# Cutting an output projection and its gate by token halves, with one half between attention blocks

## The chip, the cores and the metric

The kernel runs on one core of a Trainium2 chip. The metric is device time in microseconds, from the first instruction to the end of the program; lower is better. The profile comes from one profiled execution, and its span runs from the first to the last instruction of the program.

## The reference

One layer of a hybrid decoder trunk over 1024 tokens of width 1024. With `A = 512`:

```
xn = rms_norm(x, mix_norm)
q, k, v, gate_a, u, gate_s = split(xn @ w_in)             # six parts of 512
attn = dilated_mixture_attention(q, k, v) * silu(gate_a)  # 8 heads, windows (128,1) (512,4) (2048,16)
ssm  = s5_glu(u, ...) * silu(gate_s)                      # scan, GELU, GLU with w_glu
h    = x + concat(attn, ssm) @ w_out
gate = sigmoid(rms_norm(h, ple_norm) @ w_ple_gate)
out  = h + gate * (p @ w_ple_proj)                        # p: 256 wide
```

All arithmetic is fp32 in effect: each operand of a large product is split into a rounded high part and a remainder, and three products are summed (`mm3`).

## The kernel before

Most tiles are feature major: 128 features by 512 tokens, two token halves `n`. The stages, in the order of the program: the u projection, the state space heads woven with the two gate projections (SiLU, stored to `sg_s` and `sa_s`), q and k, v, the GLU, the output projection in two parts ("s": the four ssm rows of `w_out`, both token halves; "a": the four attention rows), the statistics of h, and the embedding gate with the embedding projection.

Attention is a Python generator (L754) over eight blocks of 128 query tokens. Its loop takes 4 heads at a time in block 0, 2 in block 1 and 1 in the others, so it has 2, 4 and 8 steps a block, 54 in all. A step is: scores on TensorE into a bank "s" (L793; blocks 4 to 7 have far keys too, L750), a row minimum on VectorE (L780), Exp on ScalarE (L803), the split in two fp16 parts by VectorE, ScalarE and GpSimd (L807 to L810), a transposing DMA (`pt<-hl`), and the product with v on TensorE (L818, L824). At the end of blocks 2, 3, 6 and 7 the finished blocks are transposed, gated and split into `ma` (two buffers of 4x512 for each token half).

`step(n)` advances the generator n steps at the place where it is called: 8 steps in v, 5 in the GLU (`GS`), 2 or 3 after each of the 16 tiles of part "s" (`OS`, 16 + 24). Tile's scheduler makes one fixed order for each engine from priorities and its own estimate of times; `high_priority` moves instructions ahead. Semaphores do the rest: an engine that waits holds everything behind it in its order. All DMAs are issued by SP, in one order.

Part "s" evicts x + 0.5 times the product and stores it to `h_s`; part "a" loads that, adds its product and makes `hh`, `hl` (high part and remainder of h) and the sum of squares. `load_w` (L146) loads a 128x512 weight tile through a ring of raw buffers (`RAW`: three, and two from the GLU on), makes the high part on ScalarE (L157, L160) and the remainder on VectorE or GpSimd (L158, L161), in 8 slots each. Part "s" and part "a" have 8 such tiles each, the gate 16, the embedding projection 4. The gate multiplies each weight tile with both token halves. Large buffers of the GLU and the output projection come from one pool of six (`quad`, tag "mx"). PSUM has the banks "big" (2), "s" (3), "t" (2) and "pv" (1).

## Time and profile before

| | |
|---|---|
| time, median of 3 runs | 690.49 us (690.44 to 690.92) |
| span of the profiled execution | 686.2 us |
| TensorE matmul busy | 630.0 us (92%) |
| VectorE busy | 496.8 us (72%) |
| ScalarE busy | 289.5 us (42%) |
| GpSimd busy | 302.0 us (44%) |
| mean granted TensorE clock | 0.968 |
| DMA | 87.25 MB, mean 127 GB/s |

The profiled execution's time is its span and what lies around it; the median of the runs is 4.3 us above the span. Busy times are unions over an engine's instructions. Matmuls are pipelined, so a stretch in which TensorE is busy throughout can hold more or fewer of them; the number of matmuls stands beside it.

### The profile page before, as it was taken

The numbers are of one execution on the slowest core, as the hardware profiler recorded it, in microseconds if no ns is written. First come the engines' busy times: TensorE is split into PE (matmuls) and PEld (weight loads), VectorE is DVE, ScalarE is ACT, GpSimd is POOL, SyncE is SP. The second block draws the span as 40 slices with busy tenths as digits, with TensorE's granted clock in tenths as the row PEclk, the third lists the DMA queues.
The fourth block names the chain that finished last, engine by engine and source line by source line (L and its number), as shares of the span: only waits on it lengthen the run. The fifth ranks groups of instructions, "written<-read, shape, count | busy, mean of one in ns | idle before, by whom it ended". The sixth has DMA issues, their size and how long they took to land.

```text
span 686.2 us, 10942 instructions
## 1 busy us (share of the span) xinstructions
PE 630.0 (92%) x3836; PEld 491.9 (72%) x3836; DVE 496.8 (72%) x1126; ACT 289.5 (42%) x553; POOL 302.0 (44%) x230
## 2 busy tenths in 40 slices
PE   9997799777879999999899789889999999999997
PEld 6875577566768788877677556566677888888786
DVE  6999999899998557767553998957944766626322
ACT  7532123445576624348434646534513455113100
POOL 3433825866775224234332845422432437342641
PEclk9999899998999999999999889989999999999999
DMA  7803612323444746754661868899987243015101
GB/s 257 241 7 109 209 38 76 105 79 93 77 92 92 167 69 125 159 86 125 161 122 48 216 147 148 213 192 191 217 226 244 94 152 124 15 63 165 50 32 61
DMA packets 158119, 87.25 MB, mean 127 GB/s; under 512 B 117232, under 2 KB 130416, under 8 KB 158064
## 3 DMA queue, kind: packets, MB, share of 16 engines
q1 hardware_dynamic: 158064, 86.56, 50.7%
q8 instruction: 30, 0.49, 0.3%
q14 instruction: 25, 0.20, 0.1%
HBM read 48.81 MB, written 17.27 MB: 96 GB/s over the span
## 4 chain that ended last, share of the span: by engine, by line
PE 46%; DVE 26%; DMA 12%; issue 7%; ACT 5%; POOL 2%; SPq 1%; DVEq 0%; ACTq 0%; POOLq 0%
PE gt L108 4%; PE gt L109 4%; PE gt L107 3%; DMA wr<-in_w_in 3%; DMA pt<-hl 3%; PE oa L107 2%; PE oa L109 2%; PE oa L108 2%; DVE tmp L270 2%; PE q L109 2%; PE q L107 2%; PE q L108 2%; DVE wl L158 2%; DVE p L780 2%; PE k L108 2%
## 5 line engine op out<-in xcount | busy, mean ns | idle before, releaser
L158 POOL TENSOR_TENSOR wl<-wr,wh 128x512 fp32r<-128x512 f32 x34 | 49.4, 1457 | 67.8 <-ACT wh L157 44.5
L157 ACT ACTIVATE wh<-wr 128x512 fp32r<-128x512 f32 x68 | 41.9, 626 | 51.4 <-DMA wr<-in_w_in 22.4
L810 POOL TENSOR_TENSOR hl<-p,hl 128x384 f16<-128x384 f32 (+2 forms) x34 | 38.9, 1148 | 53.9 <-ACT hl L807 27.1
L107 PE MATMUL g<-xh,wh 128*128 128x512 f32 x128 | 52.6, 411 | 7.3 <-DVE gate L640 5.5
L109 PE MATMUL g<-xh,wl 128*128 128x512 f32 x128 | 52.5, 410 | 5.3 <-DVE wl L158 5.3
L803 ACT ACTIVATE p<-p,st 128x384 f32<-128x384 f32 (+4 forms) x64 | 39.8, 622 | 39.1 <-DVE st L780 38.9
L108 PE MATMUL g<-xl,wh 128*128 128x512 f32 x128 | 52.0, 407 | 0.0
L108 PE MATMUL gt<-hl,wh 128*128 128x512 f32 (+1 forms) x136 | 51.7, 381 | 0.0
L107 PE MATMUL gt<-hh,wh 128*128 128x512 f32 (+1 forms) x136 | 51.7, 382 | 0.0
L109 PE MATMUL gt<-hh,wl 128*128 128x512 f32 (+1 forms) x136 | 51.2, 382 | 0.0
L158 DVE TENSOR_TENSOR wl<-wr,wh 128x512 fp32r<-128x512 f32 x34 | 34.8, 1025 | 19.1 <-ACT wh L157 14.0
L1016 ACT ACTIVATE gg<-gg 128x512 f32<-128x512 f32 (+1 forms) x17 | 10.1, 605 | 67.4 <-DVE gg L270 67.2
L1018 POOL TENSOR_TENSOR gg<-gg,hs 128x512 f32<-128x512 f32 x14 | 18.0, 1290 | 43.1 <-DVE gg L270 41.5
L107 PEld LDWEIGHTS g<-xh,wh 128*128 128x128 f32 x128 | 24.6, 192 | 13.7 <-DVE gate L640 6.5
L270 DVE TENSOR_TENSOR gg<-gt,rrow 128x512 f32<-128x512 f32 (+1 forms) x17 | 10.8, 656 | 32.7 <-PE gt L109 32.6
L109 PEld LDWEIGHTS g<-xh,wl 128*128 128x128 f32 x128 | 24.7, 193 | 12.0 <-DVE wl L158 6.6
L818 PE MATMUL pv<-vv,pt 128*128 128x64 f16 x504 | 24.4, 198 | 6.3 <-DMA pt<-hl 6.2
L818 PEld LDWEIGHTS <-pt 128*128 128x128 f16 x504 | 19.0, 101 | 14.8 <-DMA pt<-hl 8.9
L107 PEld LDWEIGHTS gt<-hh,wh 128*128 128x128 f32 x136 | 25.6, 188 | 5.5
L108 PEld LDWEIGHTS gt<-hl,wh 128*128 128x128 f32 x136 | 25.6, 188 | 5.4
L109 PEld LDWEIGHTS gt<-hh,wl 128*128 128x128 f32 x136 | 25.6, 188 | 5.4
L780 DVE CUSTOM_DVE_ANT_0 p<-sc,mask,gc 128x128 f32<-128x128 f32 (+3 forms) x56 | 24.3, 458 | 6.7 <-PE sc L793 3.2
(330 smaller groups left out, 1957.2 us busy)
## 6 DMA issues: line engine op xcount, KB each, us to landing
wr<-in_w_in SPq DMA_DIRECT2D x48, 256.0 KB, 2.9
xr<-in_x SPq DMA_DIRECT2D x16, 256.0 KB, 4.7
wr<-in_w_out SPq DMA_DIRECT2D x16, 256.0 KB, 3.3
xos<-in_x SPq DMA_DIRECT2D x16, 256.0 KB, 4.0
h_s<-xos SPq DMA_DIRECT2D x16, 256.0 KB, 3.4
xoa<-h_s SPq DMA_DIRECT2D x16, 256.0 KB, 2.8
wr<-in_w_ple_gate SPq DMA_DIRECT2D x16, 256.0 KB, 3.0
out_t<-gg SPq DMA_DIRECT2D x15, 256.0 KB, 2.0
```

Source lines behind the costliest of these rows:

```text
L107: T.matmul(o, lh, rh, start=first, stop=False)
L108: T.matmul(o, lh, rl, start=False, stop=False)
L109: T.matmul(o, ll, rh, start=False, stop=last)
L157: A.activation(hi, raw, AF.Copy)
L158: E[lo_on[k % len(lo_on)]].tensor_tensor(lo, raw, hi.bitcast(F32), op=OP.subtract)
L270: V.tensor_tensor(o, x, y, op=op)
L780: V.tensor_tensor_reduce(out, sc, msk, gm, init, op0=OP.add, op1=OP.min, accum_out=acc_[:, hd:hd + 1])
L803: A.activation(pb_, pb_, AF.Exp, bias=mx[:, hc], scale=-1.0, accum_out=dn[:, hc])
L810: E[LE[b][h0 % len(LE[b])]].tensor_tensor(hl[:, na:2 * na], pr_[:, 0:na], hl[:, 0:na], op=OP.subtract)
L818: T.matmul(pv[:, hd], pt[:, nf + i * nt + j + na * lp, :], vv[:, k0 + j, hd, lv, :], start=first, stop=end and not nf and j == n - 1 and l ...
L1016: A.activation(gt_, gt_, AF.Sigmoid)
L1018: (V if last else Q).tensor_tensor(gt_, gt_, hs, op=OP.add)
```

## The change

The output projection and the gate are done by token halves: `out_proj(n)` multiplies all eight rows of `w_out` in one accumulation, and `gate_half(n)` follows it. Half 0 of both is woven with the steps of attention blocks 4 to 7 (2 after each output tile, `GT` after each gate tile). Half 1 follows without attention. The ssm part is halved when it is split (`split_half`), `h_s` is gone. The embedding projection is moved ahead of the GLU, woven with 8 attention steps, and its tiles go through a DRAM buffer `e_s`. The GLU has 6 steps. The weights of the output and the gate are loaded once for each half. q and v of the first blocks get a pool of their own (`q0`), which is closed after step 22 to make room for `hh` and `hl` of one half. The buffers of tag "ev" go from 4 to 5, and the statistics are made for 4 blocks at a time.

```diff
+EVB = 5
-GB = ("big", "s", "big", "s")
+GB = (("big",) * 8, ("big", "s") * 4)
-GS = (1, 1, 1, 1, 1, 0, 0, 0)
+GS = (1, 1, 1, 1, 1, 1, 0, 0)
+PS = (1,) * 8
+GT = (3, 3, 3, 2, 2, 1, 1, 1)
+GSUM = 22
+EP = "QVQV"
-OS = (2,) * 8 + (3,) * 8
+OS = (2,) * 8 + (0,) * 8
+OB = (("big",) * 8, ("big", "s") * 4)
...
+    def split_half(hi, lo, src):
+        A.activation(hi, src, AF.Copy, scale=0.5)
+        stt(lo, src, 0.5, hi.bitcast(F32), OP.mult, OP.subtract)
...
+    pe_h, pe_l = quad("peh"), quad("pel")
+    for k in range(2):
+        for n in range(2):
+            pr_ = ld(f"pr{k}{n}")
+            with tc.high_priority(offset=FP):
+                nc.sync.dma_start(pr_, a["p"][k * P:(k + 1) * P, n * 512:(n + 1) * 512])
+                split(pe_h[:, 2 * k + n], pe_l[:, 2 * k + n], pr_, E[EP[2 * k + n]])
+    for sec in range(2):
+        wq = [load_w(wp, a["w_ple_proj"], k, sec * 512, lo=LG) for k in range(2)]
+        for fi in range(4):
+            f, fs = 4 * sec + fi, slice(fi * P, (fi + 1) * P)
+            for n in range(2):
+                o = bank("big", f"pe{f}{n}")
+                for k in range(2):
+                    mm3(o, wq[k][0][:, fs], wq[k][1][:, fs], pe_h[:, 2 * k + n], pe_l[:, 2 * k + n], k == 0, k == 1)
+                eo = ev(f"eo{f}{n}")
+                with tc.high_priority(offset=FP):
+                    A.activation(eo, o, AF.Copy)
+                    nc.sync.dma_start(e_s[f * P:(f + 1) * P, n * 512:(n + 1) * 512], eo)
+            step(PS[f])
...
+    def out_proj(n):
+        c = slice(n * 512, (n + 1) * 512)
+        ssb = hp.tile([P, 512], F32, tag="ssb", name=f"ssb{n}")
+        hh, hl = ([hp.tile([P, 512], F32R, tag=f"{x}{k}", name=f"{x}{k}_{n}") for k in range(KT)] for x in ("hh", "hl"))
         for sec in range(2):
+            w = [load_w(wp, a["w_out"], (k + 4) % KT, sec * 512, lo=LO) for k in range(KT)]
+            for fi in range(4):
+                f, fs = 4 * sec + fi, slice(fi * P, (fi + 1) * P)
+                xr = ev(f"xo{f}{n}")
                 with tc.high_priority(offset=FP):
+                    nc.sync.dma_start(xr, a["x"][f * P:(f + 1) * P, c])
+                o = bank(OB[n][f], f"o{f}{n}")
+                for k in range(KT):
...
                 with tc.high_priority(offset=FP):
+                    tt(xr, o, xr, OP.add)
+                    A.activation(hh[f], xr, AF.Copy)
+                    tt(hl[f], xr, hh[f].bitcast(F32), OP.subtract)
...
+                step(OS[8 * n + f])
+        return ssb, hh, hl
+
+    def gate_half(n, ssb, hh, hl):
+        rrow = hp.tile([P, 512], F32, tag="rrow2", name=f"rrow2{n}")
+        for sec in range(2):
+            w = [load_w(wp, a["w_ple_gate"], k, sec * 512, gain=plen[:, k:k + 1]) for k in range(KT)]
+            for fi in range(4):
+                f, fs = 4 * sec + fi, slice(fi * P, (fi + 1) * P)
+                last = n == 1 and f == KT - 1
+                es = ev(f"es{f}{n}")
+                nc.sync.dma_start(es, e_s[f * P:(f + 1) * P, n * 512:(n + 1) * 512])
+                gt_ = ev(f"gg{f}{n}")
+                for c in (slice(0, 256), slice(256, 512)) if last else (slice(0, 512),):
...
+                    if f == 0:
+                        stats(ssb, f"st2{n}", rcol[:, 0:4], rrow, 4)
+                    g = gt_[:, c]
+                    tt(g, o, rrow[:, c], OP.mult)
+                    A.activation(g, g, AF.Sigmoid)
+                    tt(g, es[:, c], g, OP.mult)
+                    for x in (hh, hl):
+                        (V if last else Q).tensor_tensor(g, g, x[f].bitcast(F32)[:, c], op=OP.add)
+                    nc.sync.dma_start(a["out"][f * P:(f + 1) * P, n * 512 + c.start:n * 512 + c.stop], g)
+                step(GT[f] if n == 0 else 0)
+
+    for n in range(2):
+        gate_half(n, *out_proj(n))
```

## Rows read from the trace of the kernel before

**Rows 1.** The page's 40 slices: busy tenths of TensorE and VectorE.
```profile
PE   9997799777879999999899789889999999999997
...
DVE  6999999899998557767553998957944766626322
```
**Rows 2.** Windows by stage: length, busy time by engine, clock, DMA share, GB/s.
```profile
317.00:374.00 57.00, 54.10 (x325) 41.71 (x325) 28.09 (x79) 25.58 (x65) 17.09 (x16) 1.00 0.51 112
374.00:429.00 55.00, 45.95 (x441) 31.36 (x439) 52.87 (x104) 33.80 (x74) 34.87 (x27) 0.88 0.75 166
429.00:472.00 43.00, 38.13 (x432) 26.48 (x433) 34.87 (x98) 18.70 (x46) 14.69 (x13) 0.88 0.89 202
472.00:500.00 28.00, 26.55 (x417) 18.38 (x418) 23.09 (x61) 13.30 (x28) 10.95 (x8) 1.00 1.14 201
500.00:520.50 20.50, 19.41 (x169) 14.99 (x168) 8.53 (x12) 5.07 (x8) 6.47 (x5) 1.00 0.83 237
520.50:572.00 51.50, 51.50 (x226) 41.47 (x225) 32.30 (x41) 23.82 (x39) 16.87 (x13) 1.00 0.43 143
```
**Rows 3.** Waits of TensorE, 374 to 430 us: total, times, longest.
```profile
PE sc L793 <- DVE st L780: 4.3, 4, 2.2
```
**Rows 4.** Waits of TensorE, 430 to 521 us.
```profile
PE pv L818 <- DMA pt<-hl: 3.8, 7, 1.4
```
**Rows 5.** Timeline of TensorE at 570 us: start, duration, instruction.
```profile
570.04 0.39 PE L107 MATMUL oa<-mah,wh 128*128 128x512 f32 x1
...
571.21 0.40 PE L109 MATMUL oa<-mah,wl 128*128 128x512 f32 x1
```
**Rows 6.** VectorE's groups, 317 to 520 us: busy, mean ns, idle before.
```profile
L158 DVE TENSOR_TENSOR wl<-wr,wh 128x512 fp32r<-128x512 f32 x11 | 11.3, 1031 | 8.1 <-PE os L108 5.2 <-ACT wh L157 3.0
L281 DVE SCALAR_TENSOR_TENSOR xos<-os,xos 128x512 f32<-128x512 f32 x15 | 10.1, 681 | 3.3 <-DMA wr<-in_w_out 1.9 <-PE os L109 1.2
L915 DVE TENSOR_TENSOR ym<-ygh,ygl 128x512 f32<-128x512 f32 x8 | 10.0, 1248 | 0.0
L737 DVE TENSOR_TENSOR msl<-ym,msh 128x512 fp32r<-128x512 f32 x8 | 8.4, 1047 | 0.0
...
L281 DVE SCALAR_TENSOR_TENSOR ym<-gm,ym 128x512 f32<-128x512 f32 x8 | 7.6, 958 | 1.2 <-ACT gm L918 1.2
...
L737 DVE TENSOR_TENSOR ygl<-yl,ygh 128x512 fp32r<-128x512 f32 x4 | 5.0, 1282 | 0.0
```
**Rows 7.** VectorE's groups, 520 us to the end.
```profile
L161 DVE SCALAR_TENSOR_TENSOR wl<-wr,plen,wh 128x512 fp32r<-128x512 f32 x16 | 16.4, 1038 | 10.1 <-ACT wh L160 10.0
L270 DVE TENSOR_TENSOR hl<-xoa,hh 128x512 fp32r<-128x512 f32 x16 | 16.1, 1004 | 9.6 <-ACT hh L966 9.6
...
L270 DVE TENSOR_TENSOR gg<-gt,rrow 128x512 f32<-128x512 f32 x15 | 9.9, 687 | 32.1 <-PE gt L109 32.0
```
**Rows 8.** ScalarE's groups over the whole span.
```profile
L1016 ACT ACT_TABLE_LOAD x1 | 1.3, 1283 | 0.0
```
**Rows 9.** Timeline of ScalarE among the state space heads.
```profile
143.27 0.63 ACT L157 ACTIVATE wh<-wr 128x512 fp32r<-128x512 f32 x1
...
145.14 1.28 ACT L601 ACT_TABLE_LOAD   x1
146.44 0.66 ACT L601 ACTIVATE ygt<-yp 128x256 f32<-128x256 f32 x2
```
**Rows 10.** The chain that ended last, gate's second section: start, duration, what.
```profile
616.49 0.73 ACT wh L160
...
631.30 0.73 ACT wh L160
```
**Rows 11.** TensorE's groups, 557 to 573 us, one line of each kind.
```profile
L107 PE MATMUL oa<-mah,wh 128*128 128x512 f32 x13 | 5.1, 395 | 0.0
L107 PE MATMUL gt<-hh,wh 128*128 128x512 f32 x11 | 4.4, 396 | 0.0
```
**Rows 12.** Timeline of VectorE at the end of the span.
```profile
682.93 0.42 DVE L1018 TENSOR_TENSOR gg<-gg,hs 128x256 f32<-128x256 f32 x1
```

More of the change, by code (lines that the diff above doesn't have):

```diff
@@ L46 @@
 LG = "QV"
-LO = {"s": "QV", "a": "QV"}
-LP = {"s": 3000, "a": 3000}
+LO = "QV"
 EM = "VVVV"
@@ L103, in hybrid_layer @@
     yg_s = dr.tile([512, S], F32, name="yg_s")
-    h_s = dr.tile([D, S], F32, name="h_s")
+    e_s = dr.tile([D, S], F32, name="e_s")
     def mm3(o, lh, ll, rh, rl, first, last):
@@ L174, in hybrid_layer, with stats @@
     rcol, rsq_, vcol = col[:, 0:NB], col[:, NB:2 * NB], col[:, 2 * NB:3 * NB]
-    def stats(ss, name, out_col, out_row):
-        t = bank("t", name + "c", (P, NB))
-        for b in range(NB):
+    def stats(ss, name, out_col, out_row, nb=NB):
+        t = bank("t", name + "c", (P, nb))
+        for b in range(nb):
             T.matmul(t[:, b:b + 1], ss[:, b * P:(b + 1) * P], ones, start=True, stop=True)
-        V.tensor_scalar(vcol, t, 1.0 / D, EPS, op0=OP.mult, op1=OP.add)
-        r = rsqrt(cp, vcol, [P, NB], "rs")
+        V.tensor_scalar(vcol[:, 0:nb], t, 1.0 / D, EPS, op0=OP.mult, op1=OP.add)
+        r = rsqrt(cp, vcol[:, 0:nb], [P, nb], "rs" if nb == NB else "rh")
         V.tensor_copy(out_col, r)
-        for n in range(2):
+        for n in range(nb // 4):
             m = bank("t", f"{name}r{n}")
@@ L458, in ev @@
     def ev(name, shape=(P, 512)):
-        return rp.tile(list(shape), F32, tag="ev", name=name, bufs=4)
+        return rp.tile(list(shape), F32, tag="ev", name=name, bufs=EVB)
     def wa(name, shape, dt=F32):
@@ L671, in halves, with vvb @@
         return buf("hl", name, (P, 10, P), F16)
-    qh, ql, ks = (at.tile([P, H, S], F16, name=n) for n in ("qh", "ql", "ks"))
+    q0p = ExitStack()
+    q0 = q0p.enter_context(tc.tile_pool(name="q0", bufs=1))
+    ks = at.tile([P, H, S], F16, name="ks")
+    qh, ql = ([p_.tile([P, H, 512], F16, name=f"{n}{i}") for i, p_ in enumerate((q0, at))] for n in ("qh", "ql"))
+    vv = [q0.tile([P, 3, H, 2, 64], F16, name="vv0"), at.tile([P, NB - 3, H, 2, 64], F16, name="vv1")]
+    def vvb(b):
+        return vv[0][:, b] if b < 3 else vv[1][:, b - 3]
     gv = b2t("prb", "gv", (P, 64), PB["prb"][0])
@@ L838, in attention @@
             yield
-    att = attention()
+    att, taken = attention(), [0]
     def step(n):
         for _ in range(n):
+            taken[0] += 1
             with tc.high_priority(offset=ATT):
                 next(att, None)
-    vv = at.tile([P, NB, H, 2, 64], F16, name="vv")
     sc_ = cp.tile([P, 12 + NB], F32, name="vscale")
@@ L946, in out_proj @@
-                    done(f, n, c, xr)
-                if part == "s":
-                    step(OS[i * 8 + f])
-    def spill(f, n, c, xr):
-        nc.sync.dma_start(h_s[f * P:(f + 1) * P, c], xr)
-    out_proj("s", a["x"], 0.5, spill)
-    step(64)
+                    tt(xr, o, xr, OP.add)
+                    A.activation(hh[f], xr, AF.Copy)
+                    tt(hl[f], xr, hh[f].bitcast(F32), OP.subtract)
+                    if f == 0:
+                        A.activation(ssb, xr, AF.Square)
+                    else:
+                        A.activation(xr, xr, AF.Square)
+                        E[SB2[f]].tensor_tensor(ssb, ssb, xr, op=OP.add)
@@ new lines, in out_proj @@
+                step(OS[8 * n + f])
[11 more added lines that the diff above has]
+                for c in (slice(0, 256), slice(256, 512)) if last else (slice(0, 512),):
+                    m = c.stop - c.start
+                    o = bank(GB[n][f] if c.start == 0 else "s", f"gt{f}{n}{c.start}")[:, 0:m]
+                    for k in range(KT):
+                        mm3(o, w[k][0][:, fs], w[k][1][:, fs], hh[k][:, c], hl[k][:, c], k == 0, k == KT - 1)
+                    if f == 0:
+                        stats(ssb, f"st2{n}", rcol[:, 0:4], rrow, 4)
[7 more added lines that the diff above has]
+                step(GT[f] if n == 0 else 0)
@@ L955, in hybrid_layer @@
+    for n in range(2):
+        gate_half(n, *out_proj(n))
+        if n == 0:
+            step(64)
+    hpx.close()
     ph2.close()
     kvp.close()
-    hp = ctx.enter_context(tc.tile_pool(name="hp", bufs=1))
-    ssb = hp.tile([P, S], F32, name="ssb")
-    plen = hp.tile([P, KT], F32, name="plen")
-    nc.sync.dma_start(plen, a["ple_norm"])
-    hh_ = [hp.tile([P, S], F32R, name=f"hh{k}") for k in range(KT)]
-    hl_ = [hp.tile([P, S], F32R, name=f"hl{k}") for k in range(KT)]
-    def finish(f, n, c, xr):
-        A.activation(hh_[f][:, c], xr, AF.Copy)
-        tt(hl_[f][:, c], xr, hh_[f].bitcast(F32)[:, c], OP.subtract)
-        if f == 0:
-            A.activation(ssb[:, c], xr, AF.Square)
-        else:
-            A.activation(xr, xr, AF.Square)
-            E[SB2[f]].tensor_tensor(ssb[:, c], ssb[:, c], xr, op=OP.add)
@@ L974, in hybrid_layer @@
-    out_proj("a", h_s, 1.0, finish)
-    rrow = hp.tile([P, S], F32, name="rrow2")
-    mpx.close()
-    ep = ctx.enter_context(tc.tile_pool(name="ep", bufs=24, side="right"))
-    def page(name, dt=F32R):
-        return ep.tile([P, 512], dt, tag="pg", name=name, bufs=24)
-    stats(ssb, "st2", rcol, rrow)
-    pp = {}
-    for k in range(2):
-        for n in range(2):
-            pp[k, n] = page(f"ph{k}{n}"), page(f"pl{k}{n}")
-            pr_ = ld(f"pr{k}{n}")
-            nc.sync.dma_start(pr_, a["p"][k * P:(k + 1) * P, n * 512:(n + 1) * 512])
-            split(*pp[k, n], pr_)
```

88 lines of the change are left out of this document (21 added, 67 removed).

## The prediction

> **What bounds the kernel now.** I read the page's 40 slices first. TensorE is full over the second half, except in the slices where attention and the GLU run, and there VectorE is full in its stead [rows 1]. The windows cut by stage give the sizes [rows 2]. From 317 us (v) to 520.5 us (end of the ssm part of the output projection) TensorE is idle for 2.90, 9.05, 4.87, 1.45 and 1.09 us, 19.4 us in all; in the next 51.5 us it has none. In two of these windows the granted clock is 0.88: 0.24 of their time at the lower level, 1.2 GHz, half speed. Both have idle time; the windows without the lower level have less or none. Its price is at most half of that time, and by TensorE's busy share 0.12 x 45.95 = 5.5 us and 0.12 x 38.13 = 4.6 us. So 29.5 us are lost between 317 and 520.5 us, 14.6 of them in the GLU's window (374 to 429) and 12.0 in that of blocks 4 to 7 (429 to 520.5). In the first, VectorE works 52.87 of 55 us and TensorE's longest wait is for the row minimum that frees a score bank [rows 3]; in the second it is for the transposed probabilities, a DMA behind VectorE, ScalarE and GpSimd [rows 4]. All that comes after is bound by TensorE's own work, which no edit here makes smaller.
>
> The change can gain only what is lost between 374 and 520.5 us, 26.6 us. It does so by giving attention more dense matmuls to hide behind.
>
> **TensorE's work, before and after.** A 512-column matmul starts every 0.23 us (five starts from 570.04 to 571.21: 0.234) [rows 5]. The projections issue as many as before: output 384, gate 384, embedding 96, GLU 96, v 192. From 317 to 520.5 us, 203.5 - 29.5 = 174.0 us are work; 480 dense matmuls (v, GLU, ssm half) take 111.8 at 0.233, so the 54 attention steps take 62.2 us, 1.15 each. Now 40 of the steps are handed to the ssm half's 192 matmuls. Afterwards:
> - v with 8 steps is as before;
> - embedding projection and GLU, 192 matmuls (44.7 us) with 14 steps (16.1): 60.8 us;
> - output and gate of token half 0, 384 matmuls (89.5) with 32 steps (36.8): 126.3 us;
> - output and gate of half 1, 89.5 us with nothing else.
>
> **VectorE's work.** Busy time from 317 to 520.5 us is 147.5 us [rows 2]. The GLU's four groups are 31.0, weight remainders 11.3, the projection's evictions 10.1 [rows 6]; left are 95.1 us, with v's remainders and the end of k in them, so at most 1.76 a step; I take 1.65, as v has at least the 8 x 0.7 us of such an eviction.
> - *Projection and GLU:* 14 x 1.65 = 23.1, GLU 31.0, ten remainders (two of p, two of the projection, two of the GLU's weights, four of w_out) 10.3: 64.4 us against TensorE's 60.8. In the GLU's window now it is 52.87 against 45.95 - 5.5 = 40.4. VectorE still leads, by 6% instead of 31%.
> - *Half 0:* 32 x 1.65 = 52.8; remainders of 4 w_out and 16 gate weights 4.1 + 16.6; evictions 5.5, remainders of h 8.0, one square sum and the half stats some 4, two multiplies per gate tile 11.0 [rows 6, 7]: 102 us against 126 (81%). In the window of blocks 4 to 7 it is 66.5 against 79.5 (84%).
>
> Removed: 16 of the 32 evictions (10.9 us of VectorE), 16 stores and 16 loads of h. Added: 32 more weight tiles (w_out and the gate's weights are read once per half), each a 256 KB load, a ScalarE copy and a remainder; 16 stores and loads of the embedding tiles, with 16 ScalarE evictions. The 8 MB more and the longer list on SP's queue I cost at nothing: half 1 moves 56 tiles of 256 KB in some 92 us, 160 GB/s, and from 500 to 520.5 us the queue moved 237 GB/s with TensorE idle 1.09 us [rows 2]. Without that cover SP would hold transposes behind weight loads, and the wait of [rows 4] would grow. GpSimd's two adds per gate tile stay two.
>
> **What of it reaches the end.**
> 1. *Projection and GLU.* VectorE's 64.4 us and some 4 for mismatches make 68.5, so 7.7 us lost where 14.6 are: **-6.9**. Bounds: 0 if VectorE binds as hard as now, -14.6. I don't take the better end, because the six big buffers get scarcer: embedding input (2) and attention output of half 0 (2, made at step 14) are in use when the GLU's inputs (4) come, so a GLU half can store nothing until its four tiles are through, with five small buffers to hold them.
> 2. *Blocks 4 to 7.* Twice as many dense matmuls per step, at the same load of VectorE. At the present share of loss (12.0 of 91.5, 13%) it would be 16.6 (+4.6), with none 0 (-12.0). I take 9: **-3.0**. The filler doubles, but the dense tiles have only the two "big" banks there.
> 3. *Section boundaries in half 1.* Eight weight slots hold one section, so the next section's weights start only as the last tile frees them, through two raw buffers. The gate stage shows the rate: three pairs from 616.49 to 631.30, 2.47 us a weight [rows 10]. A section's 96 matmuls take 22.4 us, its weights 19.7. If the four tiles of a section stand in four banks, each weight feeds 12 matmuls, 2.8 us, and nothing waits; if they run one after another, the eighth weight comes about 7 us late. Four boundaries: 0 to +28. The scheduler does put the next stage's matmuls ahead: between 557 and 573 us 13 "oa" and 11 "gt" matmuls of one kind are mixed [rows 11], and half 1 has five banks. I take 0.6 each: **+2.4**.
> 4. *Tail.* One more 256-column add behind the last product, 0.42 us [rows 12], and its hand-over: **+0.5**. The second stats chain hides behind the gate tiles in five banks, as its cover now does.
>
> Sum: -6.9 - 3.0 + 2.4 + 0.5 = -7.0. The span falls from 686.2 to 679.2; around it lie 4.3 us (median 690.49), so **683.5 us**.
>
> **Sigmoid between Exps.** The gate now starts while attention still runs. ScalarE shows a table load of 1283 ns before the first Sigmoid, after the last Exp [rows 8], and loads of that length where Gelu follows Silu; from the start of one to the next activation it is 1.30 us [rows 9]. GLU's Tanh beside Exp has none. Eight gate tiles with steps between cost up to 15 loads, 19.5 us of ScalarE in half 0. ScalarE is busy 37.1 of 91.5 us in the window of blocks 4 to 7 [rows 2]; at that rate 55 of 135 us, with 16 weight copies, 24 evictions, squares and sigmoids about 27 more (0.73 and 0.63 us each [rows 9, 10]), and the loads: 101 of 135. It has the room, so I put nothing in the sum; but the loads stand in front of an Exp for which VectorE, the transposes and a bank wait. The Trainium skill, "ScalarE: Activation LUTs", section "Table sets: the hidden batching unit", says to batch activations by set, and puts exp with tanh in one set and sigmoid as the anchor of another; that speaks against this order. Its section on what a load costs adds a drain, 2.66 us a switch, which would be 40 us of ScalarE here; the row shows 1.30 us.
>
> **Rivals.**
> - *Weights late (slower).* Point 3 at its upper end: 690.5 - 9.9 + 0.5 + 28 = 709 us. It decides from 2.35 us per boundary on. For it: two raw buffers, and every section starved at its head. Against: the mixed order [rows 11].
> - *ScalarE's table loads and the busier engines hold attention (slower).* If half of the 19.5 us reaches the path in half 0, 683.5 + 9.8 = 693 us. Against it: several steps are in flight.
> - *The GLU stays bound by VectorE (no change).* Its vector work is the same 31 us and its buffers are scarcer: point 1 gives 0, the rest -0.1: 690.4 us.
> - *Full cover (faster).* Both stages together lose 5 us: -21.6 + 2.9: 672 us.
>
> **Chances.** Forecast (676 to 689) 0.34; full cover 0.20; no change 0.10; table loads and load of engines 0.20; late weights, in part or whole, 0.16. I call anything within 0.2% (1.4 us) no change. Faster 0.54, same 0.10, slower 0.36. The range from 668 to 703 us reaches into full cover and into the late weights; the forecast's own is 676 to 689.
>
> **What would show it.** After the v stage: VectorE's busy share in the GLU's stretch (below 0.93 if point 1 holds) and the granted clock there; idle TensorE time while blocks 4 to 7 run, with its releaser; table loads at the Sigmoid's and the Exp's lines; gaps of TensorE at the heads of half 1's four sections, with a weight's remainder as releaser. The prediction is wrong if half 1 takes more than some 95 us, or if half 0 with attention takes more than 140.

## The result, and the profile after

The changed kernel takes 720.82 us (median of 4 runs, 719.52 to 723.89) where the kernel before takes 690.47 beside it (4 runs): ratio 1.0459, interval 1.0424 to 1.0495. It is slower by 30 us. The forecast was 683.5 us, its range 668 to 703. The profiled span grows from 686.2 to 719.9 us, by 33.7. That is 3 us more than the medians differ. In all runs that give both, the time is 1.7 to 2.1 us above the span, while the median of the kernel before is 4.3 above its profiled span. So its profiled execution was probably some 2 us faster than its median.

The slices of the page answer to [rows 1]; the third line is the granted clock in tenths.

```profile
PE   8996899787998999999998978999999998999995
...
DVE  5999998999995577685537669584555545344486
...
PEclk9998899999999999999999988899999999999998
```

Behind the first third VectorE is full (9 tenths or more) in one slice, 432 to 450 us, where it was in four, and TensorE is not fuller for it. The windows by stage answer to [rows 2]: v; embedding projection; GLU; output of half 0; gate of half 0 in two cuts; the rest of half 1; the tail. The columns are the window, its length, busy time and instructions of TensorE's matmuls and weight loads, VectorE, ScalarE and GpSimd, the granted clock, the DMA share and GB/s.

```profile
319.00:374.70 55.70, 53.83 (x326) 41.80 (x325) 28.13 (x79) 25.76 (x66) 17.56 (x16) 1.00 0.54 114
374.70:426.00 51.30, 42.41 (x418) 28.18 (x416) 37.83 (x100) 34.25 (x80) 24.56 (x21) 0.95 0.99 232
426.00:478.40 52.40, 47.66 (x521) 31.66 (x521) 39.79 (x90) 25.58 (x57) 25.82 (x20) 0.82 0.67 150
478.40:554.60 76.20, 75.14 (x409) 45.52 (x405) 40.82 (x83) 31.66 (x60) 24.92 (x18) 1.00 0.49 119
554.60:600.00 45.40, 41.85 (x356) 32.49 (x354) 24.43 (x43) 15.03 (x24) 16.82 (x12) 1.00 0.53 146
600.00:664.80 64.80, 61.70 (x257) 48.41 (x256) 27.88 (x36) 23.59 (x39) 29.46 (x22) 0.97 0.48 154
664.80:711.20 46.40, 46.40 (x233) 38.66 (x231) 30.99 (x47) 15.08 (x23) 17.32 (x12) 1.00 0.40 132
711.20:719.90 8.70, 0.10 (x1) 0.00 (x0) 4.58 (x7) 0.42 (x1) 3.92 (x3) 0.71 0.33 121
```

Look at the fourth line. TensorE is busy 75.14 of 76.20 us at the full clock, with 409 matmuls. 192 of them are dense ones of 512 columns, 44.9 us at 0.234 [rows 5]; the other 217 are attention's short ones and have the 30 us that are left, 0.14 each. In the kernel before, the 1322 short matmuls from v on (34 of them belong to statistics) take 66.1 us, 0.05 each (how this is counted stands below). Busy time hides this loss; the timeline shows it (start, duration, engine, line, instruction; in brackets the idle time before it). `far` are the far scores of block 7, 32 weight columns each.

```profile
519.08 0.50 PE L111 MATMUL o<-msh,wh 128*128 128x512 f32 x1
519.50 0.09 PEld L767 LDWEIGHTS <-ql 128*32 128x32 f16 x1 [0.24 <-issue]
519.50 0.23 PE L767 MATMUL far<-ks,ql 128*32 128x128 f16 x1
519.66 0.19 PEld L112 LDWEIGHTS o<-msl,wh 128*128 128x128 f32 x1
519.66 0.50 PE L112 MATMUL o<-msl,wh 128*128 128x512 f32 x1
```

From one dense matmul to the next it is 0.58 us, with one far score between, where dense ones alone start every 0.234 [rows 5]. The second weight load starts only 0.16 us after the narrow matmul. In the trace of the changed kernel 48 narrow matmuls (32 weight columns) stand alone like this, at 0.345 us each, 16.6 us: 42 far scores of block 7, 2 of other blocks, and 4 products with the values of far keys (`pv<-vc,pt`). None did before. The first expectation counts 54.

**Where the 33.7 us went.** I split each span in four: the start of v; TensorE's idle time (the gaps in front of its matmuls, summed) between there and the last matmul; its work in between; the tail behind. Of the work, one part can be told apart: for every run of attention matmuls between two dense ones, the time from dense to dense, less gaps and less 0.234, summed ("attention"; the 34 matmuls of the statistics, 3 to 4 us, are in it). The last column is half of the time at the lower clock level, 1.2 GHz, from v to the last matmul. It is no fifth part: it lies partly in the work, partly in idle time.

| kernel | time, ratio to before | span | start of v | idle | work | of it attention | tail | half of low-clock time |
|---|---|---|---|---|---|---|---|---|
| before | 690.5 | 686.2 | 317.1 | 19.5 | 344.5 | 66.1 | 5.1 | 11.9 |
| changed | 720.8, 1.0459 | 719.9 | 319.2 | 23.2 | 368.6 | 86.3 | 8.9 | 13.7 |
| e1 far grouped | 713.2, 1.0341 | 712.2 | 321.9 | 28.1 | 352.5 | 68.2 | 9.7 | 15.4 |
| e2 offset 100 | 716.6, 1.0387 | 715.3 | 318.3 | 22.9 | 364.3 | 77.8 | 9.8 | 11.9 |
| e4 spread | 722.5, 1.0426 | 712.2 | 318.0 | 27.1 | 358.2 | 74.9 | 8.9 | 8.5 |
| e6 embedding alone | 706.7, 1.0217 | 705.3 | 319.2 | 30.6 | 350.2 | 66.3 | 5.3 | 20.5 |
| e7 behind the GLU | 705.3, 1.0206 | 703.9 | 319.0 | 28.7 | 350.9 | 72.0 | 5.3 | 22.2 |
| e8 behind attention | 698.1, 1.0102 | 696.0 | 317.5 | 24.7 | 348.4 | 66.1 | 5.3 | 17.1 |
| e9 halves alone | 731.5, 1.0581 | 730.8 | 320.1 | 27.6 | 373.5 | 92.7 | 9.6 | 15.4 |
| e10 halves grouped | 718.8, 1.0437 | 714.7 | 318.0 | 30.1 | 357.6 | 74.3 | 8.9 | 17.1 |

Changed against before: start +2.1, idle +3.7, work +24.1 (of it +20.2 in attention's matmuls; the clock's column grows by 1.7), tail +3.8. The start of v differs between executions of the same program part (317.1 to 321.9), so some 2 us of it are no effect of an edit.

The waits, embedding projection and GLU first (total, times, longest), answer to [rows 3] and [rows 4]; the last line is from 554 to 612 us.

```profile
PE pv L835 <- DMA pt<-hl: 3.7, 5, 1.0
PE pe L111 <- DVE vv L285: 1.7, 1, 1.7
...
PE sc L767 <- DVE st L797: 3.4, 2, 1.9
PE glu L111 <- ACT ygh L749: 2.8, 1, 2.8
...
PE gt L111 <- ACT wh L164: 4.5, 3, 2.6
```

### The profile page after: what moved, and what is told of

Its sections match the earlier page's. It is cut to its first block, busy times and chain, and to the rows that moved or that the text cites. A ratio compares the mean times of both kernels' runs of the same rounds, so it can differ in the third digit from the quotient of the medians.

```text
span 719.9 us, 11119 instructions
## 1 busy us (share of the span) xinstructions
PE 656.3 (91%) x3836; PEld 495.2 (69%) x3836; DVE 504.2 (70%) x1150; ACT 317.3 (44%) x601; POOL 313.4 (44%) x235
## 4 chain that ended last, share of the span: by engine, by line
PE 45%; DVE 22%; DMA 14%; issue 7%; ACT 6%; POOL 4%; SPq 2%; DVEq 0%; ACTq 0%; POOLq 0%
DMA pt<-hl 4%; PE o L111 4%; PE o L112 4%; PE o L113 4%; DMA wr<-in_w_ple_gate 3%; DMA wr<-in_w_in 3%; PE sc L810 2%; PE q L113 2%; PE q L112 2%; PE q L111 2%; DVE tmp L274 2%; PE k L112 2%; PE k L113 2%; PE k L111 2%; PE g L111 2%
## 5 line engine op out<-in xcount | busy, mean ns | idle before, releaser
L162 POOL TENSOR_TENSOR wl<-wr,wh 128x512 fp32r<-128x512 f32 x44 | 62.5, 1422 | 82.5 <-ACT wh L161 67.7
L161 ACT ACTIVATE wh<-wr 128x512 fp32r<-128x512 f32 x88 | 54.2, 626 | 76.6 <-DMA wr<-in_w_in 28.3
L162 DVE TENSOR_TENSOR wl<-wr,wh 128x512 fp32r<-128x512 f32 x44 | 41.4, 943 | 37.3 <-ACT wh L161 37.1
L112 PE MATMUL g<-xl,wh 128*128 128x512 f32 x128 | 53.6, 419 | 0.0
L165 DVE SCALAR_TENSOR_TENSOR wl<-wr,plen,wh 128x512 fp32r<-128x512 f32 x32 | 29.1, 910 | 29.9 <-ACT wh L164 29.9
L113 PE MATMUL gt<-hh,wl 128*128 128x512 f32 (+1 forms) x136 | 48.7, 388 | 0.2
L164 ACT ACTIVATE wh<-wr,plen 128x512 fp32r<-128x512 f32 x32 | 23.1, 722 | 52.5 <-DMA wr<-in_w_ple_gate 32.4
L1024 POOL TENSOR_TENSOR gg<-gg,hh 128x512 f32<-128x512 f32 x15 | 21.6, 1444 | 46.5 <-DVE gg L274 46.5
L826 DVE CAST hl<-p 128x384 f16<-128x384 f32 (+2 forms) x34 | 16.8, 496 | 18.4 <-DMA pt<-hl 12.1
L112 PEld LDWEIGHTS g<-xl,wh 128*128 128x128 f32 x128 | 25.6, 200 | 5.6 <-issue 0.3
```

The costliest lines, as they stand in the source:

```text
L112: T.matmul(o, lh, rl, start=False, stop=False)
L113: T.matmul(o, ll, rh, start=False, stop=last)
L161: A.activation(hi, raw, AF.Copy)
L162: E[lo_on[k % len(lo_on)]].tensor_tensor(lo, raw, hi.bitcast(F32), op=OP.subtract)
L164: A.activation(hi, raw, AF.Copy, scale=gain)
L165: V.scalar_tensor_tensor(lo, raw, gain, hi.bitcast(F32), op0=OP.mult, op1=OP.subtract)
```

## The experiments

In the first expectations theory A is that the isolated narrow matmuls cost the time, and its rivals are that they do not; later ones name theories of their own. All times below stand beside a run of the kernel before on the same chip.

### Far scores in groups (e1)

```diff
                     far7 = bank(F7, f"far{b}{h0}")
-                    for j in range(4):
-                        far_scores(far7[:, j * P:(j + 1) * P], b, h0 + j)
+                    with tc.tile_critical():
+                        for j in range(4):
+                            far_scores(far7[:, j * P:(j + 1) * P], b, h0 + j)
```

> The changed kernel, with block 7's 64 far-score matmuls (32 columns wide) issued as two sections of 32 that the scheduler may not cut; nothing else is edited. Theory A: 54 far-score matmuls stand one by one between 512-column matmuls in the changed kernel, and each such pair takes 0.585 us where the dense one alone takes 0.234, so 18.2 us of the loss are these. In the new order 2 stay between dense matmuls: 720.8 - 15 to 17, so 704 to 706 us; a little more if the two sections themselves cost a branch. Rival B: the loss is in the weights that are read twice and in the gaps at the sections, and the single far matmuls only fill time that TensorE would have waited: 718 to 721 us.

Measured: 713.15 us (711.77 to 716.87), ratio 1.0341 [1.0300, 1.0383], between the two theories' numbers. Attention's matmuls fall from 86.3 to 68.2 us, as A says, but the time falls by 7.7 only: idle time rises by 4.9, and in this execution v starts 2.7 later. The window of the output of half 0 shows it.

```profile
479.80:546.90 67.10, 61.19 (x410) 42.84 (x398) 42.08 (x83) 30.83 (x60) 25.42 (x18) 0.95 0.56 134
```

Idle is 5.91 us where it was 1.06, and the clock 0.95 where it was 1.00. The slow alternation had covered waits that now show; the longest, 3.3 us, is for a weight's remainder (`wl`). 25 pairs of attention matmuls still stand between dense ones; they cost 10.1 us, 11.1 in the changed kernel and 2.1 (7 pairs) in the kernel before.

### The price of one isolated matmul, in the kernel before

54 extra matmuls on a small fp16 tile, into a bank that nobody reads, set by a fixed order between the dense ones of part "a" of the output projection (`mm3` with each of its three products kept in order and this behind it). One by one (p_iso32):

```diff
...
+        tc.keep_in_program_order(T.matmul(dmb[32 * c:32 * c + 32, 0:P], dm[:, 32 * c:32 * c + 32], dm, start=True, stop=True,
+                                          tile_position=(0, 32 * c)))
```

> The kernel before, with 54 extra fp16 matmuls of 32 weight columns and 128 moving columns put one by one behind the first 54 matmuls of the attention part of the output projection, in a fixed order; they write a bank that nobody reads. There TensorE has no idle time and no other stretch is touched. Theory A: 54 x 0.35 = +18.9 us, 709.4 us. Rival B: a small matmul costs what it costs in a row of its kind, 0.03 us, +1.6 us: 692 us.

Measured: 709.22 us, ratio 1.0277 [1.0258, 1.0295]; the 54 cost 18.9 us in the trace, 0.35 each. The same 54 in six rows of nine (p_batch32):

> The kernel before, with the same 54 extra matmuls at the same place, but in six rows of nine. Theory A: only the turn from dense to narrow costs, six times 0.35, and the rest some 0.03 each: +2 to +4 us, 692.5 to 694.5 us. Another theory C: it is the narrow matmul itself that is dear, wherever it stands: +19 us as in the other run.

Measured: 693.41 us, ratio 1.0043 [1.0026, 1.0060]. The timeline shows one row of nine between two dense matmuls:

```profile
520.64 0.40 PE L988 MATMUL oa<-mah,wl 128*128 128x512 f32 x1
520.97 0.34 PE L983 MATMUL dmb<-dm 128*32 128x128 f16 x9
521.24 0.50 PE L988 MATMUL oa<-mah,wh 128*128 128x512 f32 x1
```

From dense to dense it is 0.60 us, so the row of nine costs 0.36 us, as much as one narrow matmul alone; the six rows cost 2.2 us. It is the alternation that costs, not the matmul. The same one by one, but with all 128 weight columns (e3):

> The kernel before, with 54 extra matmuls of full size (128 weight columns, 128 moving columns, fp16) set one by one between the dense matmuls of the output projection, where the narrow ones of 32 weight columns cost 18.9 us. Theory A1, it is the narrow placement of the weights (a quarter of the array) that stops the next weights from loading ahead: a full-size one costs what it costs in a row, 0.05 to 0.08 us, so 54 make 3 to 4 us and the time is 693 to 695 us. Theory A2, any small fp16 matmul between two fp32 ones does it: again about 0.35 us each, 18 to 19 us, and 708 to 710 us.

Measured: 695.90 us (693.82 to 699.87), ratio 1.0077 [1.0039, 1.0114], 0.9 us above A1's range; from dense to dense the 54 cost 6.9 us, 0.13 each. The timeline of this kernel, to be held against the one of the far scores:

```profile
521.77 0.48 PE L987 MATMUL oa<-mal,wh 128*128 128x512 f32 x1
522.09 0.10 PEld L983 LDWEIGHTS <-dm 128*128 128x128 f16 x1 [0.15 <-issue]
522.09 0.23 PE L983 MATMUL dmb<-dm 128*128 128x128 f16 x1
522.09 0.20 PEld L987 LDWEIGHTS oa<-mah,wl 128*128 128x128 f32 x1
522.13 0.47 PE L987 MATMUL oa<-mah,wl 128*128 128x512 f32 x1
```

Here the dense matmul's weights load beside the small one's and the matmul follows 0.04 us behind it; with 32 columns they load only 0.16 us after the narrow one's start. So A1: narrow placement makes it dear, though a full-size one alone costs 0.13 us and not the 0.05 to 0.08 that A1 gave it. The Trainium skill, "TensorEngine Tiling (Array Packing)", section "Key Properties", says that a change of tiling mode drains TensorE; these traces agree in so far as each turn to narrow matmuls and back costs 0.35 us, however many stand in the row, against 0.13 without a change of mode.

### Where attention runs

`ATT` is the priority offset that puts attention's steps ahead. First (e2):

```diff
-ATT = 300
+ATT = 100
```

> The changed kernel with the attention steps moved ahead by 100 instead of 300 places in the scheduler's order, so that blocks 4 to 7 stay longer where the program has them; in its order no far-score matmul stands alone between dense ones, and 238 of the 320 wide score matmuls come before the output projection, where the changed kernel has 284. Theory A: the 18.2 us of the single far matmuls go, 702 us; if attention that is hidden behind the output and gate of half 0 also saves idle time in the GLU (13.6 us idle and 10.7 us of halved clock between 375 and 478 us), down to 690. Rival B: no gain from the far matmuls, 715 to 721 us.

Measured: 716.62 us, ratio 1.0387 [1.0356, 1.0417], in B's range. No far score of block 7 stands alone, as expected, but 18 products with the values of far keys do, which are narrow too, 5.8 us:

```profile
519.88 0.48 PE L113 MATMUL o<-msh,wl 128*128 128x512 f32 x1
520.29 0.20 PE L841 MATMUL pv<-vc,pt 128*32 128x64 f16 x1
520.43 0.50 PE L111 MATMUL o<-msh,wh 128*128 128x512 f32 x1
```

Attention's matmuls take 77.8 us, 8.5 less, and 4.2 us reach the end. Now `ATT = -100`, with the far scores grouped as above (e4):

> The changed kernel with the far scores of block 7 grouped by fours and the attention's priority lowered, so that by the order of instructions 160 of 320 wide score matmuls are left at the output projection's start, and 108 behind the output projection of half 0 (36 and 0 in the changed kernel). If the forecast failed only because attention had run ahead of half 0 (theory C), half 0 now hides the attention: 684 to 692 us. If the rest of the loss is in the stages themselves (theory A: the embedding projection's and the GLU's stage, the tail, stalls of TensorE on small matmuls), spreading gives little beyond the grouping: 705 to 713 us.

Measured: 722.53 us (714.22 to 724.11), ratio 1.0426 [1.036, 1.0491], above both theories' ranges. The profiled execution took 714.22 us, the least of the four, so its windows show less than the median's loss. At the start of the output projection 23 of the 64 Exp are left, and 18 at the gate's; in the changed kernel 11 and none, in the kernel before 25 at the start of part "s". Its windows: output of half 0, gate of half 0, output of half 1.

```profile
459.10:511.60 52.50, 52.50 (x311) 38.65 (x311) 27.34 (x55) 22.32 (x42) 17.74 (x14) 1.00 0.49 136
511.60:582.30 70.70, 69.06 (x517) 46.40 (x517) 46.23 (x106) 38.68 (x61) 27.04 (x20) 1.00 0.56 138
582.30:655.30 73.00, 62.54 (x542) 46.80 (x541) 38.93 (x69) 33.35 (x57) 33.30 (x23) 0.95 0.64 150
```

Half 0 has only 1.64 us of idle time there: the cover that point 2 spoke of works when attention is there to be covered. But attention now lasts until 620 us, half 1's output stands between its last steps, with 10.5 us idle, and the stretch of embedding projection and GLU has 14.3. Theory C falls: the losses change place. This order also shows the Sigmoid beside Exp (ScalarE's groups):

```profile
L821 ACT ACT_TABLE_LOAD x7 | 9.0, 1283 | 3.7 <-DVE st L797 3.6
L1022 ACT ACT_TABLE_LOAD x7 | 9.0, 1283 | 7.8 <-DVE gg L274 7.7
```

Fourteen loads, 18 us of ScalarE. Nine of them fall into the gate of half 0 (511.6 to 582.3), where ScalarE is busy 38.68 of 70.70 us and TensorE idle for 1.64 us: there their price does not reach TensorE. The Trainium skill, "ScalarE: Activation LUTs", section "Table sets: the hidden batching unit", which the prediction weighed, says to do all calls of one set ahead of the next; the trace agrees that going back and forth between Exp and Sigmoid brings a load each time.

### The embedding projection alone

The kernel before, with the block of the embedding projection, its stores to `e_s` and the loads from it as in the change, and all else as before (e6):

```diff
+    pe_h, pe_l = quad("peh"), quad("pel")
...
-                    for k in range(2):
-                        mm3(es[n], wq[k][0][:, fs], wq[k][1][:, fs], *pp[k, n], k == 0, k == 1)
+                    es.append(page(f"es{f}{n}", F32))
+                    nc.sync.dma_start(es[n], e_s[f * P:(f + 1) * P, n * 512:(n + 1) * 512])
```

> The kernel before with the embedding projection alone ahead of the GLU, as in the change, and the output projection and the gate as before. If this half of the change is what the forecast's point 1 made of it, the time falls to 682 to 686 us. If the projection only moves from a stretch without idle time to one where its matmuls take 0.28 us in place of 0.23, and the GLU waits for buffers longer (theory A), it rises by 3 to 8 us, to 693 to 698 us; no change, 689 to 692, would put all of the loss on the token halves.

Measured: 706.72 us (705.15 to 707.12), ratio 1.0217 [1.0188, 1.0246]. This part alone loses half as much as the whole change, and more than any of its theories gave. Windows: the projection, the GLU with attention, the last attention steps, part "s".

```profile
376.50:418.50 42.00, 37.19 (x320) 25.61 (x319) 30.37 (x72) 28.57 (x64) 22.20 (x19) 0.96 1.00 231
418.50:485.80 67.30, 58.56 (x831) 39.28 (x827) 60.46 (x149) 36.69 (x82) 31.14 (x25) 0.87 0.80 167
485.80:510.00 24.20, 16.89 (x201) 11.90 (x200) 18.66 (x36) 11.50 (x22) 8.98 (x6) 0.72 0.97 205
510.00:562.00 52.00, 45.49 (x202) 35.35 (x201) 13.31 (x21) 6.31 (x10) 8.99 (x7) 0.93 0.57 176
```

Attention ends at 514 us, as before (510). The GLU ends at 486 in place of 425, part "s" starts at 495 in place of 429. So the last steps stand nearly alone (7.3 us idle, clock 0.72), and most of part "s" follows when nothing is left to cover its own waits, 6.5 us, where the kernel before has no idle time from 520.5 us on [rows 2]. The same block, moved to behind the GLU (e7):

> The kernel before with the embedding projection alone moved, but to behind the GLU, where the projection ahead of the GLU measured 706.7 us. Theory P (place): ahead of the GLU it holds back the GLU's end from 425 to 486 us, so that TensorE has no output matmuls to set between the last attention steps; behind the GLU most of that is gone, 691 to 698 us. Theory D (detour): the 8 MB that go through e_s and back, and dense work among attention steps at all, are what costs: it stays at 702 to 708 us.

Measured: 705.33 us, ratio 1.0206 [1.0171, 1.0241]: no better, and in D's range. Here TensorE has nothing but attention between the GLU and the projection (428 to 442.4 us, busy 8.08 of 14.40, clock 0.73), and its longest wait, 4.9 us, is for transposed probabilities later on. And behind all of attention, between the two parts of the output projection (e8):

> The kernel before with the embedding projection alone moved to between the two parts of the output projection, behind all attention steps, with the same stores to e_s and loads from it. Theory P (place): nothing of the attention is touched, 689.5 to 693 us. Theory D (detour): the transfers cost here too, 698 us or more.

Measured: 698.14 us, ratio 1.0102 [1.0071, 1.0134], in D's range, but the transfers are not seen to cost. The gate stage, where the loads are, has no idle time (busy 87.20 of 87.20 us from 603.7 us on). The time stands where the projection starts (waits of TensorE from 520 to 700 us):

```profile
PE pe L110 <- ACT peh L739: 5.1, 3, 2.6
```

By the code, its inputs need two of the six big buffers, which part "s" holds until its end. Of the 9.8 us of span, 5.2 are idle time and 3.9 work, with 5.1 more by the clock inside it. So P's number is missed too: each place has its own wait, and the detour through `e_s` is not seen to cost. The other half of D, that dense work among attention steps costs, is not excluded: the two places among the steps lose twice as much as this one. One more trial (e15), the GLU's inputs of half 0 loaded ahead of the projection's (in the changed kernel they are loaded only from 421.1 us on, beside the last stores of `e_s`, and TensorE has attention alone from 416.7 to 426.1):

```diff
+    glu_input(0)
     pe_h, pe_l = quad("peh"), quad("pel")
...
-    for n in range(2):
-        yg.append((quad(f"ygh{n}"), quad(f"ygl{n}")))
...
+    glu_input(1)
```

> The kernel before with the embedding projection alone ahead of the GLU (706.7 us), and the GLU's inputs of half 0 loaded and split ahead of the projection's own. If late inputs of the GLU are the loss (theory I), the gap of 10 us between the last matmul of the projection and the first of the GLU closes, and the time falls by 5 to 9 us, to 698 to 702. If the loss is that attention is done with before the dense work is, and something else is late next (theory M), it stays within 3 us of 706.7 or rises.

Measured: 709.88 us, ratio 1.0282 [1.0235, 1.0328]. The gap closes (437.0 to 437.3), and theory I falls all the same, for M: the projection itself starts later (381.0 for 376.5) and takes 56 us for 42, and part "s" starves behind the GLU, where attention is done with: 15.9 us idle. The wait of SP there (497 to 565 us), and VectorE and TensorE at its end:

```profile
SPq L963 <- DMA h_s<-xos: 32.1, 12, 3.8
...
558.60 0.69 DVE L161 TENSOR_TENSOR wl<-wr,wh 128x512 fp32r<-128x512 f32 x1 [6.99 <-ACT wh L160]
...
560.01 1.28 DVE L284 SCALAR_TENSOR_TENSOR xos<-os,xos 128x512 f32<-128x512 f32 x2
560.74 0.63 PE L110 MATMUL os<-msh,wh 128*128 128x512 f32 x1 [3.83 <-DVE xos L284]
```

Part "s" has four small buffers for x. SP stands twelve times, 32 us in all, until a store to `h_s` has landed and frees one for the next load, and whatever SP issues next is behind that; in e6 it is 32.3 us (490 to 562), in the kernel before, with attention in between, 10.0 (429 to 521). VectorE stands 7 us in front of a weight's remainder, and the eviction that frees TensorE's bank is behind it in its order. So here the fixed order can be seen to pass a wait on.

The same in the changed kernel with grouped far scores (e16):

> The changed kernel with block 7's far scores grouped (713.2 us) and the GLU's inputs of half 0 ahead of the embedding projection. Theory I: 704 to 708 us. Theory M: 711 to 717 us.

Measured: 723.53 us, ratio 1.0475 [1.0442, 1.0509], against 713.15 without it. This is above both ranges, so not theory I. Idle rises to 33.7 us, and 17 narrow products with values and one far score stand alone in the new order.

### Token halves alone

The changed kernel, with the embedding projection's block (`embed`, without its attention steps) between output and gate of half 0 (e9):

```diff
...
-        gate_half(n, *out_proj(n))
+        got = out_proj(n)
+        if n == 0:
+            embed()
+        gate_half(n, *got)
```

> The changed kernel with the embedding projection taken from ahead of the GLU and put between output projection and gate of half 0: token halves without the early projection; its order of instructions has 41 narrow far scores alone between dense matmuls (48 in the changed kernel). If the two parts of the change add up (theory P), the early projection's 15 us are gone: 703 to 708 us. If the losses overlap, both being TensorE's lack of work that can be set between attention steps (theory O), less is won: 711 to 719 us.

Measured: 731.47 us, ratio 1.0581 [1.0533, 1.0629], outside both. 41 far scores and 12 narrow products with values stand alone (19.3 us). With the far scores grouped (e10):

> The same, with block 7's far scores in groups of four heads as well. If the isolated narrow matmuls are a loss of their own, 41 by 0.35 us, 14 us less than the kernel without the groups by theory P, 690 to 695 us; half of that given back as in the earlier pair (7.7 of 16): 696 to 701 us; above 703 us, token halves lose by something not named yet.

Measured: 718.80 us (716.65 to 726.91), ratio 1.0437 [1.0362, 1.0512]. Nine narrow products and one far score still stand alone. Grouping gives 12.7 us, but idle time is 30.1 us. This is not the halves alone either: in the projection's stretch (520.3 to 563.8 us) 4.1 us are idle and 5.1 go by the clock. Without these 9.2 us it would still be some 710 us (an estimate from this trace), so token halves lose without the early projection too, and the parts do not add up.

### The GLU with less VectorE

The switch loads the GLU's input a second time in place of adding its two parts on VectorE (8 adds, 10.0 us [rows 6]):

```diff
-RY = "V"
+RY = "D"
```

In the kernel before (e12):

> The kernel before, with the GLU's eight re-additions of its input (10.0 us of VectorE) replaced by eight loads of it. If VectorE binds the GLU's window, as the forecast's point 1 had it (theory V), TensorE's lost time there falls by some 5 us: 683 to 687 us. If the order of instructions and late inputs bind it (theory R), 689 to 693 us.

Measured: 692.89 us (10 runs), ratio 1.0036 [1.0012, 1.0061], in R's range: no gain, a little loss. The GLU's window is as long as it was, 55.2 us to 55 [rows 2], with VectorE busy 50.03 and TensorE 44.03:

```profile
375.60:430.80 55.20, 44.03 (x491) 30.14 (x489) 50.03 (x113) 34.96 (x79) 34.81 (x27) 0.91 1.04 217
```

More of attention has moved into that window (491 matmuls for 441), and the GLU ends at 434.8 for 425.0. Up to the end of part "s" VectorE is busy 8.1 us less (111.3 for 119.4) and the stretch is 2.0 us shorter, but then 4.1 us of idle time appear where the kernel before has 0.1, and the total stays. In the changed kernel (e13):

> The same edit in the changed kernel. Theory V: VectorE is busy 0.76 of the GLU's stretch, so little is left to gain, 717 to 720 us. Theory R: nothing, 719 to 723 us. More than 5 us less would say that VectorE's latency and not its load holds the stretch.

Measured: 718.73 us, ratio 1.0419 [1.0387, 1.0451], 2 us less than the changed kernel, within the spread of both. That is in V's range and just below R's, so this run cannot tell them apart; it excludes a gain above 5 us, the sign of VectorE's latency.

### The tail, and all mended

The tail of the changed kernel answers to [rows 12] (VectorE, and one of GpSimd's adds beside it):

```profile
711.32 1.37 DVE L1024 TENSOR_TENSOR gg<-gg,hh 128x256 f32<-128x256 f32 x1
712.72 1.37 DVE L1024 TENSOR_TENSOR gg<-gg,hl 128x256 f32<-128x256 f32 x1
714.00 0.41 DVE L274 TENSOR_TENSOR gg<-gt,rrow 128x256 f32<-128x256 f32 x1
...
715.52 0.42 DVE L1024 TENSOR_TENSOR gg<-gg,hh 128x256 f32<-128x256 f32 x1
715.98 0.42 DVE L1024 TENSOR_TENSOR gg<-gg,hl 128x256 f32<-128x256 f32 x1
...
712.36 1.44 POOL L1024 TENSOR_TENSOR gg<-gg,hh 128x512 f32<-128x512 f32 x1
```

The same add takes 1.37 us while GpSimd adds, and 0.42 when it has done. Both slow ones end 0.28 us behind the end of a GpSimd add (712.40 and 713.80 us), as if held until it was through; the last product's multiply starts at 714.00, 3 us after its matmul. First trial (e5): the last tile's sum early, and the two tiles ahead on VectorE.

```diff
+                if last:
+                    hs = ev("hs")
+                    Q.tensor_tensor(hs, hh[f].bitcast(F32), hl[f].bitcast(F32), op=OP.add)
...
-                    for x in (hh, hl):
-                        (V if last else Q).tensor_tensor(g, g, x[f].bitcast(F32)[:, c], op=OP.add)
+                    if last:
+                        tt(g, g, hs[:, c], OP.add)
+                    for x in () if last else (hh, hl):
+                        (V if n == 1 and f > 4 else Q).tensor_tensor(g, g, x[f].bitcast(F32)[:, c], op=OP.add)
```

> The changed kernel, with the sum of hh and hl of the last tile made early on GpSimd into a buffer of its own, so that one add of VectorE is left in each half of the last tile, and the adds of the two tiles ahead of it on VectorE in place of GpSimd. If VectorE's adds at 1.37 us beside GpSimd's set the tail (theory A), the tail falls from 8.8 to 5 or 6 us and the time by 3 to 4: 716 to 718 us. If the tail is set by the transfers out (theory B), it stays within 1 us of 720.8.

Measured: 720.25 us, within 1 us as B has it; tail 7.4 us: the adds of the tiles ahead now fill VectorE, at 1.6 us for one of 512 columns beside GpSimd. Second trial (e11):

```diff
+                hs = (ssb if last else ev(f"hs{f}")) if n == 1 and f > 5 else None
+                if hs is not None:
+                    Q.tensor_tensor(hs, hh[f].bitcast(F32), hl[f].bitcast(F32), op=OP.add)
...
+                    if hs is not None:
+                        tt(g, g, hs[:, c], OP.add)
```

> The changed kernel with the sum of hh and hl of the last two tiles of half 1 made on GpSimd while their matmuls run, and one add each on VectorE behind them; GpSimd has nothing left to do in the tail. If VectorE's adds at 1.37 us beside GpSimd's set it (theory A), the tail is 5 to 6 us in place of 8.8 and the adds of 256 columns take some 0.43 us: 717 to 718.5 us. If the half as long last tile and the transfers set it (theory B), the tail stays above 7 us.

Measured: 722.43 us (719.25 to 724.27); tail 7.3 us, above 7 as B has it. But GpSimd was still at work on older tiles until 717.4 us, so the load was not out of the way: in this kernel's tail one add of 256 columns takes 1.15, again ending 0.28 us behind GpSimd's, and the next 0.42.

```profile
716.55 1.15 DVE L274 TENSOR_TENSOR gg<-gg,ssb 128x256 f32<-128x256 f32 x1
...
718.08 0.42 DVE L274 TENSOR_TENSOR gg<-gg,ssb 128x256 f32<-128x256 f32 x1
```

That GpSimd's backlog slows VectorE's adds is shown in both traces; what a tail free of it would give is not, and 1.5 us do not show in the medians. B's transfers are part of the tail: behind VectorE's last instruction 3.5 us pass, 2.9 in the kernel before. The Trainium skill, "SBUF — State Buffer", section "SBUF: two separate sides", describes a lock between a VectorE operation with two SBUF inputs and a GpSimd operation that reads SBUF. The trace agrees: VectorE's slow adds end with GpSimd's, and the multiply, which reads PSUM, takes 0.41 us beside one (714.00).

The diffs of the grouping, of `ATT = 100` and of the second trial together (e14):

> The changed kernel with block 7's far scores grouped, the tail's sums early and the attention's priority offset 100 in place of 300: no isolated far score between dense matmuls by the order of instructions. Theory A, the named losses add: 720.8 less 7.7 (grouping, as measured), 3.5 (tail) and 4 (offset, as measured) is 705 to 707 us. If grouping and offset win the same thing twice: 708 to 712 us. Below 690, token halves would pay once mended; no theory says so.

Measured: 711.57 us (709.93 to 717.65), ratio 1.0321 [1.027, 1.0372], in the second range: the gains do not add up. No far score stands alone, but 17 narrow products with values do, 5.5 us (in the profiled execution, of 717.65 us). No version run here beats the kernel before.

## Why the prediction was wrong

The sign was wrong. By its own points, with lost time as it was reckoned there (idle, and the missing share of the clock times busy time):

1. **Projection and GLU, forecast -6.9, measured +9.7.** Lost are 8.89 + 4.74 us idle and 0.05 x 42.41 + 0.18 x 47.66 = 10.7 by the clock, 24.3, where 14.6 were lost and 7.7 forecast. The step that failed is "VectorE's 64.4 us and some 4 for mismatches": it took VectorE for the bound. VectorE did get room (0.74 and 0.76 of the two windows, where below 0.93 was asked for), and TensorE lost more. Its waits are for inputs (`ygh`, `vv`), banks and transposes, and taking 10 us off VectorE won nothing in the kernel before (e12), while e13 leaves it open for the changed one (2 us, within the spread). So the rival that VectorE binds the GLU falls too.
2. **Blocks 4 to 7, forecast -3.0, measured +17.8.** Two steps failed. "32 steps" did not run in half 0: 11 of 64 Exp were left at its start, since the order made with `ATT = 300` runs attention ahead of the dense work (with -100, in e4, 23 are left). And a step does not cost "1.15 each" wherever it stands: its matmuls, cut into pieces between dense ones, took 20.2 us more. 48 isolated narrow ones take 16.6 us, which at 0.05 each would be 2.4. p_iso32 and p_batch32 show that price alone. Idle and clock were right by accident, 7.7 + 1.9 = 9.6 us, where I took 9. Output and gate of half 0 took 141 us (478.5 to 619.5), over the 140 that was named.
3. **Section boundaries, forecast +2.4, measured about 0.** Half 1 has no idle time from 619.8 to the last matmul, 91.4 us, as worked out. Weights come late at the gate of half 0 only, 4.5 us, counted under 2. The rival of late weights falls. The 8 MB more, costed at nothing, do not show in the transposes: TensorE waits 4.9 us for them from 374.7 to 554.6 us, where it was 5.6 from 374 to 520.5.
4. **Tail, forecast +0.5, measured +3.8.** The add itself is 0.42 us when alone; what was missed is that GpSimd's adds of the tiles ahead run into it when the last tile is half as long.

With v's window (-1.0) and its start (+2.1) this is 32.4 of 33.7 us. Of the 18.1 us that grouping takes out of attention's matmuls, 7.7 reached the end. The 4.3 us around the span, which the prediction added, probably hold some 2 us by which the profiled execution was shorter than the median.

The rival of the table loads fell twice: the changed kernel has no load more than the kernel before, one ahead of the first Sigmoid, because Exp was done before the gate began, and in e4 nine fall into half 0's gate without a wait of TensorE worth naming. "Full cover" needed the loss to be a lack of dense work. More of it did not help: e6 and e7 hand attention 22 us of it, and lose 15 and 14 us by their ratios.

What stays open is one cause for the losses of the embedding projection. Each trace names other waits, and e15 shows that mending one brings the next. One link can be read in the traces: with the projection ahead, the GLU ends 61 us later (e6), attention is all but over when part "s" runs, and the waits for its four small buffers come to light. That the fixed order decides everywhere is argued from this and not shown. Token halves without any other move were not reached: e9 and e10 move the embedding projection too.

## What to carry to other kernels

Before giving an engine with waits more work to fill them, find out whether it waits for lack of work or because its order puts a late instruction in front; in e6 and e7 more dense work among attention's steps cost 14 to 15 us, and moving one stage shifted the inputs behind it. Price a matmul by its neighbours: keep narrow ones, set at a part of the array (`tile_position`), in rows, and in a stretch that reads as fully busy count the matmuls. Look up in the order of instructions, not in the program, where the work that is to be covered runs.

## What the hardware showed that was not expected

One matmul of 32 weight columns between two full-array ones costs 0.35 us, and nine in a row cost 0.36 together (p_iso32, p_batch32); one of 128 columns costs 0.13 (e3). VectorE's add of 128x256 with both inputs in SBUF took 0.42 us alone and 1.15 to 1.37 beside GpSimd's adds, ending 0.28 us behind them.
